# Second layer's MLP: the last four single tiles of the first chunk as seven half-size products

## The chip, the core and the metric

The kernel runs on one core of a Trainium2 chip. TensorE (PE) multiplies and writes to PSUM, VectorE (DVE) and ScalarE (ACT) do elementwise work, GpSimd (POOL) computes a little and issues transfers, SyncE (SP) issues transfers. The metric is the device time of one execution in microseconds; the kernel before takes 854.51 us, the median of three runs (853.74 to 854.65).

## What is computed

A decoder of two layers over 512 tokens of 1024 features, all in float32. Layer 0 mixes tokens by pooling, layer 1 by a gated unit; each then has an MLP of 4096 hidden features.

```python
for i in range(DEPTH):
    ...
    x = x + g1[:, None, :] * y
    h = modulate(rmsnorm(x, norm_mlp_g[i]), sh2, sc2)
    x = x + g2[:, None, :] * sq_relu_mlp(h, mlp_w1[i], mlp_w2[i])

def sq_relu_mlp(h, w1, w2):
    return jnp.square(jax.nn.relu(h @ w1)) @ w2
```

## The kernel before

**Products in three passes.** An operand is split into a high and a low half: ScalarE rounds it to the matmul type (`split`, L176; `parts`, L637), VectorE subtracts (L177, L638). `mm3` multiplies low by high, high by low and high by high (L187, L188, L190), so every product of two 128-row pieces costs three matmuls, all adding up in one PSUM bank.

**The MLP.** `mlp(i, ...)` handles the 4096 hidden features in four chunks of 1024, each in two quarters of 512. The up-projection `h @ w1` is made in one of two ways:

- A *single tile* (`f_prep`, `f_run`) makes 128 hidden features for all 512 tokens, 256 tokens at a time, over 8 pieces of the contraction. `put` applies relu (L678) and squares (L666).
- A *quarter by seven products* (`s_prep`, `s_run`) treats A (the normed tokens) as 2x2 blocks of 256 tokens by 512 input features, and B (a quarter of `w1`) as 2x2 blocks B11, B12, B21, B22 of 512 input by 256 hidden features. Instead of eight block products there are seven, of sums of blocks: product 1 is A11·B11, 2 is A12·B21, the others (5, 6, 3, 7, 4) use sums. Each has 2 x 4 x 3 matmuls of 256 columns. They run in the order 1, 5, 6, 3, 7, 2, 4.

Products 1, 6, 7 and 4 add up in one bank (`IN_X`, `XS`); 5 and 3 in a second and 2 in a third (`ZS`). After 1, 6 and 5 ScalarE copies the unfinished bank to `g` (L823); after 2, 3 and 7 VectorE combines bank and `g` (L826, L828, L830), then relu (L831) and square (L666).

The weights of a quarter are four loads of 512 KB (`blk`, SP's queue) into tiles of `w4`, which has three buffers. VectorE adds blocks (L787) for products 5 and 6; the sums for 7 and 4 are accumulating transfers on POOL's queue (L782). Each product's weight is then split (L176, L177).

The operands of 5, 6, 3 and 7 are sums of A's blocks: `a_sums(0)` to `a_sums(3)` make them in place in `h32` and split them into `as` tiles (one in `hx`, two in the buffers of the residual `x0`, `x1`, which are spilled to memory before) and, for product 7, into the part of `hb` that holds A21.

**Order.** `units` lists the steps: single tiles ("f"), products ("s"), down-projection steps of a chunk ("p") and of the last chunk ("q"). The loop prepares up to four steps ahead (`ahead`, which limits weight tiles), starts the pieces of `extra` (modulation columns, each tied to a number in the list), runs a step on TensorE, and goes on. TensorE's order is written by hand; on the other engines the framework's scheduler fixes an order when the kernel is built, and each works through it in sequence. In chunks made by products the list has the products between the down-projection steps of the chunk before, so that a p step lies between any two products of the group 1, 6, 7, 4.

In layer 1, `first1` makes the first four tiles of chunk 0 together: the first 256 tokens of each, then the other 256, while the second half of the tokens is still being normed (`normed(1, 1, 1)`). Then come the single tiles 4 to 7, then the products of chunk 1. `a_sums(0)` to `a_sums(3)` are called after tiles 4, 5, 6 and 7.

Of the kernel before, what the change touches and what calls it, by code (L numbers as in the profile page):

```python
# [14 lines left out]
P = 128  # L15
D = 1024
S = 512
KD = D // P
# [27 lines left out]
def c_g(n, k):  # L46
    return 24 * n + 16 + k
# [34 lines left out]
def decoder_kernel(ctx: ExitStack, tc: tile.TileContext, xtok, vecs, rows, fgrow, ada0, adag, ada1, pool_w, w1s, w1, w1f, w1b, w2, w2e, w_v, w_u, w_o, wsT, lnp, bs, out):  # L82
# [40 lines left out]
    mods = [cp.tile([P, 48], F32, name=f"mods{i}") for i in range(2)]  # L123
# [33 lines left out]
    def raw4(src):  # L157
        r = w4.tile([P, D], F32, name="raw", tag="w4")
        nc.sync.dma_start(r, src)
        return r  # L160
# [9 lines left out]
    def split(r, n=1):  # L170

        h, l = wpair()
        latest[0] = h
        for q in range(n):
            c = slice(D // n * q, D // n * (q + 1))
            A.activation(h[:, c], r[:, c], AF.Copy)  # L176
            V.tensor_tensor(l[:, c], r[:, c], f32(h[:, c]), ALU.subtract)  # L177
        return h, l
# [60 lines left out]
    def spread_cols(cols, name):  # L239

        po = bank("pb")[0:KD, 0:P]
        T.transpose(po, cols, ident)
        r = sm.tile([KD, P], F32, name="line", tag="line", bufs=1)
        A.activation(r, po, AF.Copy)
        line = dram.tile([KD, P], F32, name=name)
        G.dma_start(line, r)
        gb_[0] = big.tile([P, D], F32, name="gb", tag="gb")
        G.dma_start(gb_[0], line.rearrange("(o k) p -> o (k p)", o=1).to_broadcast([P, D]))
# [26 lines left out]
    with (  # L275
# [14 lines left out]
        m = band.rearrange("p n g w -> p (n g) w")  # L290
        G.affine_select(out=m, in_=m, compare_op=ALU.is_ge, fill=0.0, base=0, pattern=[[0, 8], [1, W]], channel_multiplier=-1)
        for g in range(4):
            m = band[:, :, g]
# [288 lines left out]
        for op in WORK.split():  # L582
            on_v, op = op.endswith("V"), op.rstrip("V")
            kind, d = op.rstrip("0123456789"), [int(c) for c in op if c.isdigit()]
# [42 lines left out]
    ORDER = (1, 5, 6, 3, 7, 2, 4)  # L627
# [10 lines left out]
        V.tensor_tensor(o[1], a, f32(o[0]), ALU.subtract)  # L638


    FROM = (2, 1)

    def mlp(i, first, extra, last, ending):

# [2 lines left out]
        with (  # L647
# [37 lines left out]

            def f_prep(u):
                c, f = u
                return split(raw4(w1[8 * c + f] if i == 0 else w1f[8 * c + f]))

            def f_run(u, w):  # L690
                c, f = u
# [41 lines left out]
            def a_sums(step):  # L733


                def a(r, j):
                    return h32[0][:, 4 * j : 4 * j + 4, 256 * r : 256 * r + 256]

                def operand(pool, tag):
                    t = pool.tile([P, 2, 4, 256], F32R, name="as", tag=tag)  # L740
                    return t[:, 0], t[:, 1]

                def minus(o, p, q):
                    V.tensor_tensor(o, p, q, ALU.subtract)

                first, half = slice(0, 256), slice(256, 512)
                if step == 0:
                    sums_a.update({1: H(slice(0, 4), first), 2: H(slice(4, 8), first), 4: H(slice(4, 8), half)})
                    shift(hx, LINE - GAP)
                    minus(a(1, 1), a(1, 0), a(1, 1))  # L750
                    m, o = 5, operand(hx, "hx")
                elif step == 1:
                    minus(a(1, 1), a(1, 1), a(0, 0))
                    m, o = 6, operand(big, "x0")
                elif step == 2:
                    minus(a(0, 0), a(0, 0), a(1, 0))
                    V.tensor_tensor(a(1, 1), a(1, 1), a(0, 1), ALU.add)
                    m, o = 3, operand(big, "x1")
                else:
                    m, o = 7, H(slice(0, 4), half)  # L760
                parts(o, a(0, 0) if m == 7 else a(1, 1))
                sums_a[m] = o
# [2 lines left out]

            def quad_at(c, j):

                return 2 * (c - FROM[i]) + j + i * 2 * (4 - FROM[0])

            def blk(c, j, r, n):  # L770
                if (c, j, r, n) not in blks:
# [212 lines left out]
                    ending()  # L984

            done = first(put)
            units = [("f", (0, f)) for f in range(done, 8)]
            for c in range(3):
                if c + 1 < FROM[i]:
                    fs, lead, step = [("f", (c + 1, f)) for f in range(8)], 3, (1, 1, 1, 1, 0, 1, 0)  # L990
                else:
                    fs, lead, step = [("s", (c + 1, j, m)) for j in range(2) for m in ORDER], 2, (1, 2, 3, 2, 2, 2, 0)
                units += fs[0:lead]
                fs = fs[lead:]
                for m, n in zip(ORDER2, step):
                    units.append(("p", (c, m)))
                    units += fs[0:n]
                    fs = fs[n:]
# [7 lines left out]

            def ahead(n):

                if i == 0 and ("s", (FROM[0], 0, 1)) not in units[: n + 5]:
                    return min(n + 3, len(units))  # L1010
                m, s = n + 1, items(*units[n])
                while m < len(units) and m < n + 5:
                    s += items(*units[m])
                    if s > 5 and m > n + 1:
                        break
                    m += 1
                return m

            ready = {}
            extra, at = list(extra), 0  # L1020
            for n, (kind, u) in enumerate(units):
                for m in range(n, ahead(n)):
                    if m not in ready:
                        ready[m] = prep[units[m][0]](units[m][1])
                while at < len(extra) and extra[at][0] <= n:
                    extra[at][1]()
                    at += 1
                if i == 0 and n in A_PARTS:
                    a_parts(A_PARTS.index(n))
                narrow[:] = [units[n + 1 : n + 2] and (units[n + 1][0] in "sf" or i and units[n + 1] == ("q", (1, NT - 1)))]  # L1030
                run[kind](u, ready[n])
                if i and kind == "f":
                    a_sums(u[1] - 4)
                if u == (3, 1, 4):
                    reload()

# [66 lines left out]
    def modulation_late(q, n, get, wait=4):  # L1103

        r = []
        return [(n, lambda: r.append(ada_load(ada1[q], get))), (n + wait, lambda: ada_tile(*column_at(q), r[0], True))]
# [20 lines left out]
    with (  # L1127
# [39 lines left out]
        u, gt, wu = {}, {}, {}  # L1167
# [100 lines left out]
            V.tensor_scalar(X(t)[:, S:c0], X(t)[:, S:c0], r, None, ALU.mult)  # L1268
            nc.sync.dma_start(out[t, :, 1], X(t)[:, S:D])

    ex = [x for q in range(8) for x in modulation_late(48 + q, 8 + 5 * q, late_gb if q == 0 else get_gb)]
    ex += [(58, lambda: spread_cols(mods[1][:, c_g(1, 0) : c_g(1, 0) + KD], "gain1"))]
    mlp(1, first1, ex, last1, lambda: None)


# [11 lines left out]
def _lay_out(inp):  # L1287
    import numpy as np

    def f(name):  # L1290
        return np.asarray(inp[name], dtype=np.float32)

    def cols(v):
        return v.reshape(-1, P).T

    def fmajor(w, ct):

        return w.reshape(KD, P, -1, ct).transpose(2, 1, 0, 3).reshape(-1, P, KD * ct)

    def halves(w):  # L1300

        return w.reshape(4, 2, P, 2, S).transpose(3, 0, 2, 1, 4)

    order = _ada_columns()
    d = {}
    d["xtok"] = f("x")[0].reshape(NT, P, D)
    adab = f("ada_b").reshape(2, 48, P)[:, order]
    d["vecs"] = np.concatenate([cols(v) for v in (f("c"), adab, f("norm_mix_g"), f("norm_mlp_g"))], axis=1)
    d["rows"] = np.stack([f("c")[0], adab[0, 16:24].reshape(-1), f("pool_scale")[0]])
    d["fgrow"] = f("final_g")  # L1310
    aw = f("ada_w").reshape(2, D, 48, P)[:, :, order]

    v0 = aw[0].transpose(1, 2, 0)
    d["ada0"] = np.concatenate([v0[0:16], v0[24:40]] + [v0[16 + 2 * g : 18 + 2 * g] for g in GT])
    d["adag"] = aw[0][:, 16:24].reshape(2, 4, P, 4, 256).transpose(3, 0, 2, 1, 4)[GM]
    d["ada1"] = np.concatenate([v0[40:48], aw[1].transpose(1, 2, 0)])
    d["pool_w"] = f("pool_w")[0].reshape(8, P, 256).transpose(1, 0, 2)
    w1 = f("mlp_w1")
    d["w1s"] = w1[0].reshape(KD, P, -1)[:, :, 0 : P * SWEEP]
    d["w1"] = fmajor(w1[0][:, : 2 * D], P)  # L1320
    d["w1f"] = fmajor(w1[1][:, :D], P)

    w1b = np.concatenate([w1[0][:, 2 * D :], w1[1][:, D:]], axis=1)
    d["w1b"] = w1b.reshape(2, 4, P, 10, 2, 256).transpose(3, 0, 4, 2, 1, 5).reshape(10, 2, 2, P, D)

    w2 = f("mlp_w2").reshape(2, 4, 2, 4, P, 2, S)
    d["w2"] = w2[:, 0:3].transpose(0, 1, 2, 5, 4, 3, 6)
    d["w2e"] = np.stack([halves(w[3 * D :]) for w in f("mlp_w2")])
    win = f("sgu_w_in")[0]
    d["w_v"] = halves(win[:, D:])  # L1330
    d["w_u"] = fmajor(win[:, :D], P)
    d["w_o"] = halves(f("sgu_w_out")[0])
    d["wsT"] = f("sgu_w_s")[0].transpose(2, 0, 1)
    d["lnp"] = np.concatenate([f("sgu_ln_g")[0], f("sgu_ln_b")[0]])
    d["bs"] = f("sgu_b_s")[0].reshape(-1)
    return {k: np.ascontiguousarray(v) for k, v in d.items()}
# [17 lines left out]
```

## Time and profile before

| what | value |
|---|---|
| median of three runs | 854.51 us |
| profiled execution, its own time | 854.5 us |
| its span, first to last instruction | 852.6 us |
| granted TensorE clock, mean | 0.997 |
| matmuls | 5116 |
| moved by DMA | 182.34 MB, mean 214 GB/s |

The profile gives busy times of the engines, the chain of work that ended last, who waited for whom, and the timeline, all in microseconds from the start of the span. Matmuls overlap in the pipeline: a row's duration is longer than the distance from one matmul's start to the next, and that distance is what one costs. Buffer numbers are left out of the names: `po` and `pm` are PSUM banks, `wh` and `wl` the halves of a weight, `raw` a loaded weight block, `h` the normed tokens (`h32`), `hb` their halves, `as` the halves of a sum of A's blocks, `g` hidden features. SPq and POOLq are transfers issued by SP and POOL.

### The profile page before, as it was taken

The page shows a single profiled execution, that of the slowest core. Times are in us where ns is not written, and L with a number is a line of the kernel's source. Part 1 is how long each engine was busy: PE and PEld are TensorE (multiplying, and loading weights), DVE is VectorE, ACT ScalarE, POOL GpSimd, SP SyncE. Part 2 cuts the span into 40 slices and gives each one's busy share as a digit, 9 for nine tenths or more (in the row PEclk, how much of TensorE's full clock was granted, in tenths as well). Part 3 has the DMA queues.
Part 4 walks back from the last instruction along what each step waited for, and adds up shares of the span by engine and source line. Part 5 has one row for each costly group of instructions (what it writes and reads, how often), then busy time and mean ns, then how long its engine had stood idle before and what let it go on. Part 6 is the DMA issues. An engine that isn't in the chain of part 4 may idle for free.

```text
span 852.6 us, 13079 instructions
## 1 busy us (share of the span) xinstructions
PE 839.5 (98%) x5116; PEld 747.5 (88%) x5116; DVE 686.2 (80%) x914; ACT 484.8 (57%) x716; POOL 65.5 (8%) x89
## 2 busy tenths in 40 slices
PE   8999999999999999999999999999999999999996
PEld 7778899998999998888888888999999999999885
DVE  6889897688898988767897866777788988887855
ACT  5286875565656577247333226666766666566521
POOL 3000000010101110010020001010101000111001
PEclk9999999999999999999999999999999999999998
DMA  9959955788898776724745636947888788786302
GB/s 351 417 226 324 347 191 179 222 203 216 215 283 231 224 205 224 269 97 165 264 168 172 217 129 221 322 94 197 205 247 217 218 212 244 180 178 230 129 25 98
DMA packets 43218, 182.34 MB, mean 214 GB/s; under 512 B 4859, under 2 KB 5011, under 8 KB 36118
## 3 DMA queue, kind: packets, MB, share of 16 engines
q1 hardware_dynamic: 35282, 137.72, 44.1%
q0 software_dynamic: 7440, 41.43, 24.0%
q10 hardware_dynamic: 436, 2.37, 0.8%
q8 instruction: 40, 0.66, 0.3%
q14 instruction: 20, 0.16, 0.1%
HBM read 175.19 MB, written 6.30 MB: 213 GB/s over the span
## 4 chain that ended last, share of the span: by engine, by line
PE 92%; DMA 4%; ACT 1%; DVE 1%; issue 1%; SPq 0%; POOLq 0%; POOL 0%; DVEq 0%; ACTq 0%
PE po L187 17%; PE po L190 17%; PE po L188 17%; PE pm L188 12%; PE pm L190 12%; PE pm L187 12%; DMA wh<-in_ada 2%; DMA wl<-in_ada 1%; DMA ada<-in_adag 1%; PE po L1192 1%; ACT sq L315 1%; PE px L1073 1%; PE po L611 0%; PE po L614 0%; PE po L612 0%
## 5 line engine op out<-in xcount | busy, mean ns | idle before, releaser
L187 PE MATMUL po<-hb,wl 128*128 128x256 f32 (+1 forms) x697 | 204.8, 294 | 0.2 <-DVE wl L177 0.2
L188 PE MATMUL po<-hb,wh 128*128 128x256 f32 (+1 forms) x696 | 204.1, 293 | 0.0
L190 PE MATMUL po<-hb,wh 128*128 128x256 f32 (+1 forms) x696 | 204.0, 293 | 0.0
L177 DVE TENSOR_TENSOR wl<-raw,wh 128x1024 fp32r<-128x1024 f32 (+1 forms) x122 | 145.5, 1195 | 45.5 <-ACT wh L176 45.2
L176 ACT ACTIVATE wh<-raw 128x1024 fp32r<-128x1024 f32 (+1 forms) x122 | 126.0, 1038 | 91.8 <-PE pm L190 42.3
L187 PEld LDWEIGHTS po<-hb,wl 128*128 128x128 f32 x697 | 130.9, 188 | 4.7 <-DVE wl L177 0.6
L190 PEld LDWEIGHTS po<-hb,wh 128*128 128x128 f32 x696 | 130.7, 188 | 4.1
L188 PEld LDWEIGHTS po<-hb,wh 128*128 128x128 f32 x696 | 130.8, 188 | 3.9
L190 PE MATMUL pm<-wh,oh 128*128 128x512 f32 (+1 forms) x375 | 131.1, 367 | 0.0
L188 PE MATMUL pm<-wl,oh 128*128 128x512 f32 x336 | 130.9, 390 | 0.0
L187 PE MATMUL pm<-wh,ol 128*128 128x512 f32 x336 | 130.8, 389 | 0.0
L190 PEld LDWEIGHTS pm<-wh,oh 128*128 128x128 f32 x375 | 70.4, 188 | 14.8
L215 DVE SCALAR_TENSOR_TENSOR ada<-ada,cb 128x1024 f32<-128x1024 f32 x56 | 68.1, 1218 | 10.1 <-DMA ada<-in_ada 8.7
L187 PEld LDWEIGHTS pm<-wh,ol 128*128 128x128 f32 x336 | 63.1, 188 | 11.8
L188 PEld LDWEIGHTS pm<-wl,oh 128*128 128x128 f32 x336 | 63.0, 188 | 11.6
L177 DVE TENSOR_TENSOR wl<-bt,wh 128x1024 fp32r<-128x1024 f32 x48 | 58.3, 1220 | 15.9 <-ACT wh L176 15.9
L187 PE MATMUL po<-as,wl 128*128 128x256 f32 x240 | 66.6, 278 | 0.0
L188 PE MATMUL po<-as,wh 128*128 128x256 f32 x240 | 66.4, 277 | 0.0
L190 PE MATMUL po<-as,wh 128*128 128x256 f32 x240 | 66.3, 276 | 0.0
L176 ACT ACTIVATE wh<-bt 128x1024 fp32r<-128x1024 f32 x48 | 50.4, 1058 | 20.5 <-PE pm L190 10.7
L177 DVE TENSOR_TENSOR wl<-b,wh 128x1024 fp32r<-128x1024 f32 x36 | 43.6, 1222 | 16.1 <-ACT wh L176 16.0
L1050 ACT ACTIVATE tmp<-x 128x512 f32<-128x512 f32 (+1 forms) x25 | 15.3, 612 | 61.9 <-DVE x L1046 56.1
(220 smaller groups left out, 1558.1 us busy)
## 6 DMA issues: line engine op xcount, KB each, us to landing
ada<-in_ada SPq DMA_DIRECT2D x72, 512.0 KB, 4.7
raw<-in_w1b SPq DMA_DIRECT2D x40, 512.0 KB, 5.3
b<-in_w SPq DMA_DIRECT2D x18, 1024.0 KB, 6.8
bt<-in_w POOLq DMA_DIRECT2D x16, 1024.0 KB, 8.8
raw<-in_w1b POOLq DMA_DIRECT2D x20, 512.0 KB, 5.7
raw<-in_w2e SPq DMA_DIRECT2D x16, 512.0 KB, 3.9
bt<-in_w SPq DMA_DIRECT2D x6, 1024.0 KB, 6.0
b<-in_w POOLq DMA_DIRECT2D x6, 1024.0 KB, 9.4
```

Source lines behind the costliest of these rows:

```text
L176: A.activation(h[:, c], r[:, c], AF.Copy)
L177: V.tensor_tensor(l[:, c], r[:, c], f32(h[:, c]), ALU.subtract)
L187: T.matmul(o[:, c], wl, mh[:, c], start=first and not c.start, stop=False, **kw)
L188: T.matmul(o, wh, ml, start=False, stop=False, **kw)
L190: T.matmul(o[:, c], wh, mh[:, c], start=False, stop=last and c.stop is None, **kw)
L215: V.scalar_tensor_tensor(r, r, 1.0, cb, ALU.mult, ALU.mult, accum_out=pmv[i, b][:, j : j + 1])
L315: A.activation(j, X(t)[:, c], AF.Square, scale=D**-0.5, accum_out=out)
L1050: A.activation(tmp, xt, AF.Square, scale=D**-0.5, accum_out=s[:, len(cs) : len(cs) + 1])
L1073: T.transpose(px[:, 256 * q + P * r : 256 * q + P * r + P], xs[r][:, P * (k + q) : P * (k + q) + P], ident)
L1192: T.matmul(po[:, tok[t]], vt[t][:, ch, c0 : c0 + P], wb[:, 0, hd], start=True, stop=True)
```

## The change

In layer 1, the single tiles 4 to 7 of chunk 0 are replaced by the seven products of that chunk's second quarter. `FROM` now counts quarters made by other means (4 in layer 0, as before 2 chunks; 1 in layer 1, before 1 chunk), and the weight tables follow. `a_sums(0)` and `a_sums(1)` are called before the list starts, `a_sums(2)` and `a_sums(3)` after its first two steps. The list of layer 1 is three steps longer (seven for four), and the numbers to which the modulation pieces are tied are raised by three.

```diff
-    FROM = (2, 1)
+    FROM = (4, 1)
...
-                return split(raw4(w1[8 * c + f] if i == 0 else w1f[8 * c + f]))
+                return split(raw4(w1[8 * c + f]))
...
-                return 2 * (c - FROM[i]) + j + i * 2 * (4 - FROM[0])
+                return 2 * c + j - FROM[i] + i * (8 - FROM[0])
...
-            units = [("f", (0, f)) for f in range(done, 8)]
+            units = [("s", (0, 1, m)) for m in ORDER] if i else [("f", (0, f)) for f in range(done, 8)]
             for c in range(3):
-                if c + 1 < FROM[i]:
+                if 2 * (c + 1) < FROM[i]:
...
-                if i == 0 and ("s", (FROM[0], 0, 1)) not in units[: n + 5]:
+                if i == 0 and ("s", (2, 0, 1)) not in units[: n + 5]:
...
             extra, at = list(extra), 0
+            if i:
+                a_sums(0)
+                a_sums(1)
             for n, (kind, u) in enumerate(units):
...
                 run[kind](u, ready[n])
-                if i and kind == "f":
-                    a_sums(u[1] - 4)
+                if i and n < 2:
+                    a_sums(n + 2)
...
-    ex = [x for q in range(8) for x in modulation_late(48 + q, 8 + 5 * q, late_gb if q == 0 else get_gb)]
-    ex += [(58, lambda: spread_cols(mods[1][:, c_g(1, 0) : c_g(1, 0) + KD], "gain1"))]
+    ex = [x for q in range(8) for x in modulation_late(48 + q, 11 + 5 * q, late_gb if q == 0 else get_gb)]
+    ex += [(61, lambda: spread_cols(mods[1][:, c_g(1, 0) : c_g(1, 0) + KD], "gain1"))]
...
-    d["w1f"] = fmajor(w1[1][:, :D], P)
+    d["w1f"] = fmajor(w1[1][:, :S], P)
...
-    w1b = np.concatenate([w1[0][:, 2 * D :], w1[1][:, D:]], axis=1)
-    d["w1b"] = w1b.reshape(2, 4, P, 10, 2, 256).transpose(3, 0, 4, 2, 1, 5).reshape(10, 2, 2, P, D)
+    w1b = np.concatenate([w1[0][:, 4 * S :], w1[1][:, S:]], axis=1)
+    d["w1b"] = w1b.reshape(2, 4, P, 11, 2, 256).transpose(3, 0, 4, 2, 1, 5).reshape(11, 2, 2, P, D)
```

## The prediction

> **What bounds the kernel now.** I read the page first (busy shares, granted clock, the chain that ended last), then TensorE's own waits in the second layer's MLP, then the stretch of the four single tiles by engine, and last the timelines of VectorE, ScalarE and the queues around it.
>
> ```profile
> span 852.6 us, 13079 instructions
> PE 839.5 (98%) x5116; PEld 747.5 (88%) x5116; DVE 686.2 (80%) x914; ACT 484.8 (57%) x716; POOL 65.5 (8%) x89
> PEclk9999999999999999999999999999999999999998
> PE 92%; DMA 4%; ACT 1%; DVE 1%; issue 1%; SPq 0%; POOLq 0%; POOL 0%; DVEq 0%; ACTq 0%
> ```
>
> TensorE is busy in 98% of the span, holds 92% of the chain, and its clock is full. TensorE's waits from 520 to 640 us are one row:
>
> ```profile
> PE po L187 <- DVE wl L177: 0.2, 1, 0.2
> ```
>
> So nothing but matmuls sets the time there: a matmul taken away shortens the kernel by its spacing, and a wait put in lengthens it. The spacing, from the chain in order of time (start, us, what); the same line comes back after three matmuls:
>
> ```profile
> 549.66 0.11 PE po L190
> 550.00 0.11 PE po L190
> ```
>
> 0.34 us for three 128x256 matmuls: 0.113 us each, though one row lasts 0.28. The four tiles lie between these two rows of TensorE's timeline (first matmul of tile 4; first of the next chunk's first product):
>
> ```profile
> 549.61 0.28 PE L187 MATMUL po<-hb,wl 128*128 128x256 f32 x1
> 571.37 0.28 PE L187 MATMUL po<-hb,wl 128*128 128x256 f32 x1
> ```
>
> 21.76 us, 192 matmuls of 0.113. The busy times in that stretch (PE, PEld, DVE, ACT, POOL, each with its count; then clock, DMA share, GB/s):
>
> ```profile
> 549.50:571.30 21.80, 21.80 (x195) 21.80 (x194) 15.45 (x14) 13.45 (x19) 1.71 (x2) 1.00 0.47 128
> ```
>
> VectorE has 6.4 us free, ScalarE 8.4. That is the cover the change draws on.
>
> **The change part by part.** *Removed.* A single tile issues 2 x 8 x 3 = 48 matmuls, a product 2 x 4 x 3 = 24. 192 become 168: 24 x 0.113 = **-2.72 us**. Seven products of 2.72 us, if none waits, start at 549.61 (product 1), 552.33 (5), 555.05 (6), 557.77 (3), 560.49 (7), 563.21 (2) and 565.93 (4), and end at 568.65.
>
> *Added.* Three more weight splits (seven for four), two sums of weight blocks on VectorE (L787), two accumulating transfers on POOL's queue, three copies of unfinished products on ScalarE (L823) and three additions on VectorE (L826, L828, L830). The sums of A's blocks are the same, earlier. Durations:
>
> ```profile
> 548.70 1.22 DVE L744 TENSOR_TENSOR h<-h 128x1024 f32<-128x1024 f32 x1
> 549.84 1.22 DVE L177 TENSOR_TENSOR wl<-raw,wh 128x1024 fp32r<-128x1024 f32 x1
> 550.97 1.22 DVE L638 TENSOR_TENSOR as<-h,as 128x1024 fp32r<-128x1024 f32 x1
> 596.92 0.67 DVE L830 TENSOR_TENSOR g<-g,po 128x512 f32<-128x512 f32 x1
> ```
> ```profile
> 542.93 1.06 ACT L176 ACTIVATE wh<-raw 128x1024 fp32r<-128x1024 f32 x1 [3.46 <-DMA raw<-in_w1f]
> 543.90 1.04 ACT L637 ACTIVATE as<-h 128x1024 fp32r<-128x1024 f32 x1
> 546.27 0.62 ACT L666 ACTIVATE g<-g 128x512 f32<-128x512 f32 x1
> 546.79 0.59 ACT L678 ACTIVATE g<-po 128x512 f32<-128x512 f32 x1
> 577.01 0.60 ACT L823 ACTIVATE g<-po 128x512 f32<-128x512 f32 x1 [0.85 <-PE po L190]
> ```
>
> Back to back, 1024 columns take VectorE 1.14 us from start to start and ScalarE 0.96; 512 columns take ScalarE 0.52. VectorE gains 5 x 1.14 + 3 x 0.6 = 7.5 us against 6.4 free, in a stage that is to be 2.7 shorter; ScalarE 3 x 0.96 + 3 x 0.52 = 4.4. VectorE is over-full there unless it works ahead, so I follow both queues in the order in which the changed program issues them.
>
> *Two waits that the single tiles didn't have.* Products 1, 6, 7 and 4 add up in one PSUM bank. After 1 and after 6 ScalarE copies the bank out, and VectorE reads it after 7: the next of the four can't start before that read. In the other chunks a down-projection step stands between any two of them; in the new first chunk at most one other product does. And the blocks of a weight have three buffers: the fourth block (B21) is loaded into the buffer of B22, only when B22 is split.
>
> *VectorE up to product 6.* Its place before the stage:
>
> ```profile
> 538.99 1.30 DVE L638 TENSOR_TENSOR hb<-h,hb 128x512 fp32r<-128x512 f32 x2 [0.66 <-ACT hb L637]
> 540.32 1.22 DVE L744 TENSOR_TENSOR h<-h 128x1024 f32<-128x1024 f32 x1
> 544.03 1.23 DVE L177 TENSOR_TENSOR wl<-raw,wh 128x1024 fp32r<-128x1024 f32 x1 [2.48 <-ACT wh L176]
> 545.17 1.22 DVE L638 TENSOR_TENSOR as<-h,as 128x1024 fp32r<-128x1024 f32 x1
> ```
>
> The sums can't begin before 540.3, when the second half of the tokens is normed; the first weight block lands at 542.9 in either kernel, for its load has the old one's place, size and wait. From 545.17 VectorE then works without a break: low half of operand 5, weight sum 5, two differences of A, low half of weight 5, low half of operand 6, weight sum 6, a sum of A, low half of operand 7, low half of weight 6. Weight 5 is ready at 545.17 + 4 x 1.14 + 1.22 = 550.95, in time for 552.33. Weight 6 is the tenth: 545.17 + 9 x 1.14 + 1.22 = **556.65**, wanted at 555.05.
>
> *ScalarE up to product 6.* The high half of weight 6 needs weight sum 6, done at 545.17 + 6 x 1.14 + 1.22 = 553.23. Behind it stand a square, the high halves of weights 3 and 7, and only then the copy of product 1: 553.27 + 0.96 + 0.52 + 2 x 0.96 = 556.67, done at 557.27. Product 6 starts at 557.3 instead of 555.05: **+2.3 us**, most of it the copy behind the splits. Bounds: 1.6 (VectorE alone) to 2.5. Operand 3 (VectorE's third piece behind weight 6) is done at 545.17 + 12 x 1.14 + 1.22 = 560.07, when product 6 ends: **+0.1**.
>
> *Product 7.* B22 is split at 557.8 and SP issues B21 then. ScalarE's next two operations are the high halves of weights 2 (B21) and 4 (an accumulating transfer issued at 556.7), and the copy of product 6 stands behind both. What 512 KB take to land, each row from a window with that issue alone:
>
> ```profile
> raw<-in_w1b SPq DMA_DIRECT2D x1, 512.0 KB, 3.3
> raw<-in_w1b SPq DMA_DIRECT2D x1, 512.0 KB, 4.8
> raw<-in_w1b SPq DMA_DIRECT2D x1, 512.0 KB, 5.7
> raw<-in_w1b POOLq DMA_DIRECT2D x1, 512.0 KB, 5.6
> raw<-in_w1f SPq DMA_DIRECT2D x1, 512.0 KB, 8.3
> ```
>
> 3.3 with nothing beside it, 4.8 and 5.7 with others in flight, 8.3 under several 1 MB loads. Here one accumulating transfer was issued 1.2 us before and one load follows 1.1 us later: I take 4.6, nearest to 4.8. B21 lands at 562.5, the two splits take until 564.4, the copy until 565.0: product 7 starts at 565.1 where TensorE is free at 562.8: **+2.3**. With 3.3 the accumulating transfer (556.7 + 5.6 = 562.3) ends last: 563.95, +1.15. With 5.7: +3.4.
>
> *Product 4.* VectorE's subtraction after product 7 (L830) is queued behind a weight sum of the next quarter, whose block takes B21's buffer: issued at 562.5 + 1.1 + 1.2 = 564.9, landed 3.3 to 4.8 later, plus 1.14 and 0.67: 570.0 to 571.5, where TensorE is free at 565.1 + 5.44 = 570.5. 0 to +1.0; I take **+0.3** (4.0 us, between the two rows).
>
> *At nothing.* Four loads of 512 KB replace four; the additions L826 and L828 and the squares are on no product's path; the new start numbers of the modulation pieces (11 and 61 for 8 and 58) keep their places in a list that is three longer; the weight table only changes its cut. The down-projection step that follows wants its weights at 573.2 + 5.44 = 578.7; VectorE is through with them five pieces behind L830, near 576.5: were those 2 us gone, each us later would cost one.
>
> *Sum.* -2.72 + 2.3 + 0.1 + 2.3 + 0.3 = +2.3 us. The profiled execution took 854.5 us (span 852.6 and 1.9 around it), as the median of the three runs, 854.51: **856.8 us**. With every cost at its low end +0.1 (-2.72 + 1.6 + 0.1 + 1.15), at its high end +4.3 (-2.72 + 2.5 + 0.1 + 3.4 + 1.0).
>
> **The rivals.** *All hidden, 851.8 us.* TensorE runs the seven products through and keeps the 2.72. For it: it doesn't wait anywhere in this MLP now, and its products there have the same copies. Against it: there other work stands between products that share a bank, and VectorE's ten pieces alone miss product 6 by 1.6 us. It decides if VectorE starts the chain some 2 us earlier, which the row at 538.99 speaks against. *One stall, 854.2 us.* Product 6 waits, but B21 is there early, as blocks are elsewhere: -2.72 + 2.4. Against it: B21's buffer. *Crowded loads, about 861 us.* B21 takes 8.3 instead of 4.6: product 7 loses 3.7 more, 860.5, and the next block adds some. It speaks against this that the DMA share in that stretch was 0.47. *The clock drops, about 859.5 us.* TensorE's longest pauses would be 2.3 to 2.5 us. A pause of 1.73 us in this trace left the clock at 1.00:
>
> ```profile
> 29.02 1.35 PE L431 MATMUL pg<-ada,cab 128*128 128x256 f32 x5 [1.73 <-DMA ada<-in_adag]
> 27.00:29.00 2.00, 0.30 (x2) 0.00 (x0) 2.00 (x4) 0.51 (x2) 0.00 (x0) 1.00 1.01 415
> ```
>
> Should a longer one halve it for one product, that product takes 2.7 us more. [...]
>
> **How the numbers follow.** Forecast 0.72, all hidden 0.11, one stall 0.07, crowded 0.06, clock 0.04. A measurement tells about 0.2% (1.7 us) from no change. Of the forecast's 0.72 I put 0.08 below +1.7, where the loads land in 3.3 to 3.8. Faster 0.11; within 0.2% 0.07 + 0.08 = 0.15; slower 0.64 + 0.06 + 0.04 = 0.74. The forecast's own range is 854.6 to 858.8; with one stall and the clock's case taken in, 854.2 to 859.6, which leaves out all hidden and crowded, 0.17.
>
> **What would show it.** 24 fewer matmuls, and in TensorE's waits two rows of about 2.3 us, both on ScalarE's copy (L823), for products 6 and 7; if the one at product 6 names a low half of a weight (L177) instead, VectorE set it. On ScalarE's timeline an idle time of about 3 us ahead of a split (L176), ended by the load of B21. Product 4 within 1 us, ended by L830. From the next chunk on every step shifted by one constant. Wrong, if TensorE's row of waits stays empty, if the shift is undone further on, or if the loss lies in another stage.

## The result and the profile after

| | before | after |
|---|---|---|
| median of 5 runs each, side by side (lowest to highest), us | 854.51 (853.72 to 856.12) | 858.81 (857.51 to 859.41) |
| ratio, 95% interval | | 1.0042 [1.0031, 1.0053] |
| profiled execution: time (span), us | 854.5 (852.6) | 857.5 (855.5) |

By the ratio the changed kernel is slower by 3.6 us (2.6 to 4.6); the medians lie 4.3 us apart. The page of the changed kernel, its first two lines of text and the shares of the chain that ended last:

```profile
span 855.5 us, 13056 instructions
PE 839.2 (98%) x5092; PEld 746.6 (87%) x5092; DVE 692.8 (81%) x922; ACT 488.5 (57%) x722; POOL 67.3 (8%) x91
...
PE 88%; DMA 6%; DVE 2%; ACT 2%; issue 1%; SPq 1%; POOL 0%; POOLq 0%; DVEq 0%; ACTq 0%
```

24 matmuls are gone and TensorE is busy for as long as before (839.2 for 839.5): most of what they freed came back as slower matmuls, and waits lie on top. TensorE's waits from 520 to 640 us (total, times, longest), and its first matmul of product 5 and of the next quarter's product 5:

```profile
PE po L187 <- ACT g L823: 3.8, 2, 2.1
```
```profile
552.12 0.28 PE L187 MATMUL po<-as,wl 128*128 128x256 f32 x1
577.22 0.28 PE L187 MATMUL po<-as,wl 128*128 128x256 f32 x1
```

Where the kernel before had one wait of 0.2, there are two of 2 us, both on ScalarE's copy. From product 5 to product 5 it takes 25.10 us. That is the length of the stage, as one product of 2.72 stands ahead of each end; the four single tiles took 21.76. So the stage costs **+3.34 us**; the span is 2.9 longer. The rows ahead of product 6, on VectorE, ScalarE and TensorE (start, length, idle time before it and what ended that):

```profile
555.28 3.48 DVE L177 TENSOR_TENSOR wl<-raw,wh 128x1024 fp32r<-128x1024 f32 x3
```
```profile
554.61 1.99 ACT L176 ACTIVATE wh<-raw 128x1024 fp32r<-128x1024 f32 x2
556.51 0.57 ACT L823 ACTIVATE g<-po 128x512 f32<-128x512 f32 x1
```
```profile
557.13 0.39 PE L187 MATMUL po<-as,wl 128*128 128x256 f32 x1 [2.13 <-ACT g L823]
```

The first of VectorE's three low halves is weight 6's, done near 556.5. Two high halves hold the copy of product 1 on ScalarE until 557.08, and product 6 starts 0.05 later, 2.3 us after product 5 ends (552.12 + 2.72). Product 7 in the chain of waits (start, us, what), and ScalarE's rows for it:

```profile
556.42 1.22 DVE wl L177
...
557.66 5.98 DMA raw<-in_w1b
...
563.66 2.01 ACT wh L176 x2
565.67 0.49 ACT g L823
...
566.21 0.39 PE po L187
```
```profile
563.66 2.01 ACT L176 ACTIVATE wh<-raw 128x1024 fp32r<-128x1024 f32 x2 [4.21 <-DMA raw<-in_w1b]
565.58 0.58 ACT L823 ACTIVATE g<-po 128x512 f32<-128x512 f32 x1
```

B22's split frees the buffer, B21 takes 5.98 us to land, two splits and the copy follow. Last, the stretch by windows (busy times of PE, PEld, DVE, ACT, POOL; then clock, DMA share, GB/s):

```profile
554.80:557.10 2.30, 0.20 (x2) 0.00 (x1) 2.30 (x3) 2.30 (x4) 0.30 (x1) 1.00 0.00 0
557.10:558.70 1.60, 1.57 (x13) 1.57 (x14) 1.60 (x3) 1.60 (x2) 0.54 (x1) 0.99 0.36 33
558.70:562.10 3.40, 3.40 (x18) 3.40 (x18) 3.40 (x4) 0.76 (x2) 0.00 (x0) 0.50 0.92 202
562.10:564.30 2.20, 2.20 (x21) 2.20 (x20) 0.07 (x1) 0.64 (x1) 0.00 (x0) 1.00 0.94 380
564.30:566.20 1.90, 0.20 (x2) 0.00 (x0) 1.44 (x2) 1.90 (x4) 0.00 (x0) 1.00 0.03 6
```

After the pause ahead of product 6 the clock was 0.50 for 3.4 us: a matmul started every 0.213 us, so 16 where 30 fit at 0.113 (the 18 of the row count those that reach over its edges). That slowed products 6 and 3, which would have ended at 562.6 (557.13 + 2 x 2.72), by some 1.8 us, and left 1.9 of the 3.6 us that product 7, set by B21, would have waited.

### The profile page after: what moved, and what is told of

The parts are those of the page before. It is cut to its first block, busy times and chain, and to the rows that moved or that the text cites. A ratio compares the mean times of both kernels' runs of the same rounds, so it can differ in the third digit from the quotient of the medians.

```text
span 855.5 us, 13056 instructions
## 1 busy us (share of the span) xinstructions
PE 839.2 (98%) x5092; PEld 746.6 (87%) x5092; DVE 692.8 (81%) x922; ACT 488.5 (57%) x722; POOL 67.3 (8%) x91
## 4 chain that ended last, share of the span: by engine, by line
PE 88%; DMA 6%; DVE 2%; ACT 2%; issue 1%; SPq 1%; POOL 0%; POOLq 0%; DVEq 0%; ACTq 0%
PE po L187 16%; PE po L190 16%; PE po L188 16%; PE pm L188 12%; PE pm L190 12%; PE pm L187 12%; DMA wl<-in_ada 2%; DMA wh<-in_ada 1%; DMA raw<-in_w1s 1%; PE po L1195 1%; PE px L1076 1%; DMA ada<-in_ada 1%; DMA raw<-in_w1b 1%; ACT sq L315 1%; ACT wh L176 0%
## 5 line engine op out<-in xcount | busy, mean ns | idle before, releaser
L187 PE MATMUL po<-hb,wl 128*128 128x256 f32 (+1 forms) x665 | 196.1, 295 | 1.7 <-ACT g L823 1.7
L188 PE MATMUL po<-hb,wh 128*128 128x256 f32 (+1 forms) x664 | 195.3, 294 | 0.0
L190 PE MATMUL po<-hb,wh 128*128 128x256 f32 (+1 forms) x664 | 195.1, 294 | 0.0
L177 DVE TENSOR_TENSOR wl<-raw,wh 128x1024 fp32r<-128x1024 f32 (+1 forms) x125 | 148.8, 1195 | 43.6 <-ACT wh L176 43.4
L176 ACT ACTIVATE wh<-raw 128x1024 fp32r<-128x1024 f32 (+1 forms) x125 | 128.9, 1038 | 91.7 <-PE pm L190 41.1
L187 PEld LDWEIGHTS po<-hb,wl 128*128 128x128 f32 x665 | 124.8, 188 | 6.3 <-ACT g L823 1.9
L190 PEld LDWEIGHTS po<-hb,wh 128*128 128x128 f32 x664 | 124.7, 188 | 4.1
L188 PEld LDWEIGHTS po<-hb,wh 128*128 128x128 f32 x664 | 124.8, 188 | 3.9
L187 PE MATMUL po<-as,wl 128*128 128x256 f32 x264 | 74.2, 281 | 2.1 <-ACT g L823 2.1
L188 PE MATMUL po<-as,wh 128*128 128x256 f32 x264 | 73.8, 279 | 0.0
L190 PE MATMUL po<-as,wh 128*128 128x256 f32 x264 | 73.6, 279 | 0.0
L187 PEld LDWEIGHTS po<-as,wl 128*128 128x128 f32 x264 | 50.3, 190 | 2.4 <-ACT g L823 2.3
```

Of the source, the lines that this page charges most:

```text
L187: T.matmul(o[:, c], wl, mh[:, c], start=first and not c.start, stop=False, **kw)
L188: T.matmul(o, wh, ml, start=False, stop=False, **kw)
L190: T.matmul(o[:, c], wh, mh[:, c], start=False, stop=last and c.stop is None, **kw)
```

## The experiments

Each kernel is the changed one with the edit shown. "Stage" is the length from product 5 to product 5 in its profile, to be read against 21.76 before; the ratio is to the kernel before, run on the same chip in the same comparison, where that took 855.6 to 856.1 us. A profile is one execution, the ratio is over several; executions of one kernel lie up to 4 us apart (the kernel before 854.1 to 858.0 in these comparisons), so a stage and a ratio need not agree to 1 us.

| kernel | stage, us | ratio to before, 95% |
|---|---|---|
| e1_again (no edit) | 24.54 | 1.0044 [1.0029, 1.0059] |
| e2_b21_own | 24.29 | 1.0031 [1.0020, 1.0042] |
| e5_fresh_bank | 23.98 | 1.0045 [1.0030, 1.0060] |
| e8_defer | 21.87 | 1.0167 [1.0151, 1.0182] |
| e9_short_3 | 22.98 | 1.0004 [0.9995, 1.0013] |
| e10_short_own_3 | 21.77 | 0.9992 [0.9983, 1.0001] |
| e3_p_between | 23.9 without the step put in | 1.0016 [1.0007, 1.0025] |
| e4_both | 24.0 without the step put in | 1.0012 [1.0002, 1.0022] |
| e13_own_late | 22.80 | 1.0000 [0.9991, 1.0010] |
| e13_short_own_late_3 | 21.64 | 1.0000 [0.9991, 1.0008] |
| e15_copy_first | 24.46 | 1.0035 [1.0023, 1.0048] |
| e19_in_order | 20.76 | 1.0144 [1.0125, 1.0163] |

**The changed kernel once more** (e1_again).

> The changed kernel once more, unedited. In its first profile (857.5 us, the lowest of its five runs) TensorE paused 2.3 us ahead of product 6 and 2.0 us ahead of product 7, and the granted clock was 0.50 for 3.4 us after the first pause only; that slow stretch lay in time that product 7 spent waiting for B21 anyway. Theory 'queues' (product 6 waits for ScalarE's copy, product 7 for B21's buffer): the same two pauses again, 857.5 to 858.5 us unless a clock drop falls where nothing hides it. Rival 'clock' (the halved clock sets the loss): slow stretches after both pauses in a profile of a run near 859, that is 1.6 us more than the first profile for a second stretch.

TensorE's waits (of over 0.2 us), two pieces of the chain and one window:

```profile
PE po L187 <- ACT g L823: 4.8, 2, 3.3
```
```profile
558.16 5.89 DMA raw<-in_w1b
...
566.08 0.49 ACT g L823
```
```profile
563.10:566.60 3.50, 0.26 (x3) 0.07 (x1) 1.43 (x2) 2.49 (x3) 0.00 (x0) 1.00 0.49 193
```

Here the clock stayed at 1.00, through a pause of 3.4 us, and the profiled execution takes 858.0 us beside 857.5: product 7 starts when B21 has come, however fast products 6 and 3 ran. In these two executions the clock is not where the loss comes from. For those without a trace that is open. The five of this run have a mean granted clock of 0.998, 0.996, 0.995, 0.992 and 0.994 and take 858.01, 858.61, 858.92, 859.30 and 859.86 us; the kernel before has 0.997 on average, and its times do not follow the clock. So up to 2 us of the slower executions, an estimate from the 1.9 between these five, may be drops that nothing hides.

**B21 in its own buffer** (e2_b21_own).

```diff
-                    blks[c, j, r, n] = raw4(w1b[quad_at(c, j), r, n])
+                    if (i, c, j, r, n) == (1, 0, 1, 1, 0):
+                        blks[c, j, r, n] = ada_load(w1b[quad_at(c, j), r, n], get_gb)
+                    else:
+                        blks[c, j, r, n] = raw4(w1b[quad_at(c, j), r, n])
```

> B21 of the new quarter gets a buffer of its own (the free gain tile), so its load no longer waits for B22's split. Queues: the copy of product 6 no longer waits for B21; what is left is the accumulating transfer for weight 4 (issued at 556.7, 5.6 to 5.9 us), so product 7 starts near 564.3 instead of 566.2: 1.5 to 2 us less than the changed kernel, about 857 us. Rival 'clock': the pause ahead of product 6 and the slow stretch behind it stay, and without the wait for B21 they are what sets product 7 (564.2): about the same 857, but then the chain of waits names TensorE's slow matmuls and no transfer. Rival 'over-full VectorE': no change, 858.8, since VectorE's work is the same.

Product 7's wait is gone, product 6's grew. TensorE's wait, the transfer that stopped ScalarE (issue, KB, us to landing) and ScalarE behind it:

```profile
PE po L187 <- ACT g L826: 3.5, 1, 3.5
```
```profile
raw<-in_w1b POOLq DMA_DIRECT2D x1, 512.0 KB, 10.3
```
```profile
558.08 1.06 ACT L176 ACTIVATE wh<-raw 128x1024 fp32r<-128x1024 f32 x1 [3.53 <-DMA raw<-in_w1b]
559.05 0.58 ACT L826 ACTIVATE g<-po 128x512 f32<-128x512 f32 x1
```

The buffer was free early, so SyncE issued B21 ahead of one of the 1 MB loads of the down-projection. The 1 MB accumulating transfer that depends on that load went out at 547.0 instead of 542.3, and weight 7's transfer beside it took 10.3 us. ScalarE stood 3.5 us before weight 7's split, with the copy of product 1 behind it. The clock's drop is not hidden here: it was 0.50 for 3.41 us from 559.15 on, and product 6 took 4.19 us where product 7 of the changed kernel, which follows a pause at full clock, takes 2.85. Products 3 and 7 follow without a wait, so some 1.3 us of this stage are the clock's; to that extent the rival 'clock' was right. The earlier load and the drop together cost most of what was saved. 1.5 to 2 us less than the changed kernel were forecast; the ratio is lower by 0.0011, 0.9 us, which the intervals do not tell from nothing.

**A bank of its own for product 6** (e5_fresh_bank). Product 6 starts a new bank; product 1 is thereby left out of three of the quarter's four output blocks.

```diff
-                start, stop = m in (1, 5, 2), m in (4, 3, 2)
+                start, stop = m in (1, 5, 2) or (i, c, j, m) == (1, 0, 1, 6), m in (4, 3, 2)
```

> Product 6 of the new quarter starts a fresh PSUM bank, so it doesn't wait for the copy of product 1; product 1 is left out of three of the quarter's four output blocks. Queues: product 6 then waits for the low half of its weight alone, 1.6 to 1.8 us instead of 2.3; product 7 still waits for B21, so the time stays that of the changed kernel, 858.8 within 0.5. Rival 'clock': if the shorter pause spares the clock, 1.6 us less; if the clock falls all the same, no change. Rival 'over-full VectorE': no change.

```profile
556.14 0.35 PE L187 MATMUL po<-as,wl 128*128 128x256 f32 x1 [0.50 <-DVE wl L177]
565.63 0.39 PE L187 MATMUL po<-hb,wl 128*128 128x256 f32 x1 [3.28 <-ACT g L823]
```

Product 6 no longer waits for the copy, only 0.5 us for its weight (1.6 to 1.8 were expected; in this execution VectorE's pieces came 0.5 us earlier and TensorE 0.5 later than in the changed kernel's profile), and product 7 waits the whole rest for B21 and its copy. The ratio is that of the changed kernel: the first wait alone is worth nothing.

**The 1 MB loads later** (e8_defer). The down-projection's first two loads wait for a write that ScalarE makes from the latest split.

```diff
+                if (i, c) == (1, 0) and not chain:
+                    A.activation(t[:, 0, 0:1], f32(latest[0])[:, 0:1], AF.Copy)
                 nc.sync.dma_start(t, w2[i, c, r, n])
```

> The two 1 MB loads of down-projection weights that run ahead of the new quarter's blocks (issued near 527, landed at 538 and 541.5) are held back until the weights of a later step are split. Queues: B11 lands some 3 to 4 us earlier (539 instead of 542.7), VectorE's chain of ten pieces begins by as much earlier, and product 6 doesn't wait, or under 0.5 us; no slow clock behind it. Product 7 still waits for B21, now from a B22 that is split some 2.5 us earlier: about 2.3 to 3 us less than the changed kernel, 856 us. Rival 'over-full VectorE': the work is the same but begins earlier, the same sign, so this run tells only where the pause goes. Rival 'clock': the slow stretch goes with the pause; the gain over the changed kernel is at most 1.6 us beyond what B21 allows.

The stage lost its first wait and took 21.87 us. But the loads came too late for the steps that they feed; TensorE's waits from 520 to 640 us (those of over 0.2), with clock drops of 6.83 and 3.41 us behind the two longest (mean granted clock 0.991):

```profile
PE pm L187 <- ACT wh L176: 7.3, 2, 4.3
PE po L187 <- ACT g L823: 2.2, 1, 2.2
PE pm L188 <- DVE wl L177: 1.5, 2, 0.8
```

**Weights prepared two units ahead** (e9_short_3).

```diff
+                if i and n < 6:
+                    return n + 3
                 m, s = n + 1, items(*units[n])
```

> For the first six units of the second layer the weights are prepared only two units ahead instead of up to four, so that ScalarE's copies of products 1 and 6 are queued ahead of the weight splits that are not yet wanted. Theory (the waits of products 6 and 7 come from the order in ScalarE's queue, and behind it B21): product 6 waits for its own weight's low half on VectorE, about 1.6 us instead of 2.3; product 7 no longer stands behind B21's split; B21, issued near 557.7 and landing 6 us later, is wanted only by product 2, which then starts near 565.7 to 566 instead of 568.9. The stage costs -2.7 + 1.6 + 0.9 + 0.5 = about +0.3, against +3.3 in the changed kernel: about 855 us, 2.5 to 3 us less than the changed kernel. Rival (the buffer of B21 sets the end of the stage, whoever waits for it): product 4 or the next quarter takes over what product 7 gave back, and the time stays within 1 us of the changed kernel. What would show it: ScalarE's copy (L823) gone from TensorE's waits, a low half (L177) in its place.

```profile
PE po L187 <- DVE wl L177: 2.2, 2, 1.3
PE po L187 <- DVE g L830: 0.5, 1, 0.5
```

The copy is gone from TensorE's waits and low halves stand in its place, for product 6 (1.1 us) and for product 2, which needs B21; product 4 waits 0.5 for VectorE's subtraction of product 7. The edit changes when weights are prepared, and with it the order on ScalarE and on VectorE, and adds or removes no work. It takes 0.0038 of the ratio, 3.3 us, from the changed kernel, where 2.5 to 3 us were forecast. The stage is only 2.1 us shorter (1.6 beside e1_again); no drop of the clock follows its pauses, the longest 1.3 us, which may be the rest.

**Both, first form** (e10_short_own_3): the edits of e2_b21_own and e9_short_3.

> The short preparation of the kernel before, and B21 in a buffer of its own. Theory (two causes, ScalarE's order and B21's buffer): only product 6's wait for its weight is left, 1.6 us, as the late accumulating transfer that stopped ScalarE when B21 alone had its own buffer now stands behind the copy of product 1: the stage costs -2.7 + 1.6 + 0.3 = -0.8, about 853.5 to 854 us beside 854.5 of before. Rival (the second buffer takes SyncE's queue: its issue waits for the buffer and holds the loads behind it): weight 7 lands near 558 and the waits move on to products 7 and 4, 1 to 2 us each, and the time is that of e9_short_3 or more.

```profile
560.29 0.38 PE L187 MATMUL po<-as,wl 128*128 128x256 f32 x1 [1.52 <-ACT g L826]
```

Product 6 waits 0.4, product 7 not at all; product 3 waits 1.5 for the copy of product 5, which stands behind the split of the late weight 7. That is the rival's wait, on a product that it did not name. The time is near that of the kernel before: the interval, -1.5 to +0.1 us, holds the theory's -0.8 as well as no change, and the stage, 21.77 us for 21.76, speaks for the latter.

**A down-projection step between products 5 and 6** (e3_p_between), and with B21 in its own buffer (e4_both). The down-projection steps that follow are taken from `order` instead of `ORDER2`, and at product 4 weights are prepared two units ahead.

```diff
+                order = ORDER2
+                if i and c == 0:
+                    units.insert(2, ("p", (0, 1)))
+                    order, step = ORDER2[1:], (1, 2, 3, 2, 2, 2)
...
+                if units[n] == ("s", (0, 1, 4)):
+                    return n + 3
```

> The first down-projection step of the layer is moved from behind the seven products to a place between products 5 and 6; the buffers and the sums stay. Theory (the waits come because too little work stands between products that share a bank): the copy of product 1 and weight 6 have 5.4 us more, so product 6 doesn't wait, and B21 has as much more ahead of product 7; in exchange the down-projection step may wait up to 3 us for its own operand's split on VectorE, which is over-full there. The stage costs between -2.2 and +0.5, so 852.3 to 855 us. Rival (VectorE's amount of work sets the stage, not the order): the wait only moves to the down-projection step and the time stays within 1 us of the changed kernel's.

> The down-projection step between products 5 and 6, and B21 in a buffer of its own. Theory of the two causes: as e3_p_between, and what was left there ahead of product 7 is gone: at most 1 us less than e3_p_between. Rival (SyncE's queue is held by the issue for the second buffer): the accumulating transfer of weight 7 is late, near 558, but with 5.4 us more in hand product 7 does not notice, and the time is the same as e3_p_between's within 0.5 us.

TensorE's waits in e3_p_between (of over 0.2 us):

```profile
PE pm L187 <- DVE ol L638: 4.0, 2, 2.6
PE po L187 <- ACT g L823: 1.6, 1, 1.6
```

With the step between them product 6 waits for nothing, but the step waits 2.6 us for its own operand's low half, on VectorE, and product 7 still 1.6. The step after the stage waits 1.4 more. e3_p_between lies between its two theories: 0.0026 of the ratio, 2.2 us, below the changed kernel, and above the forecast. The distance between the products matters, and VectorE could not supply the step that was put there in time. In e4_both the step waits 0.5, but product 7 waits 2.3 for the copy of product 6, which stands behind the split of weight 4; that weight's accumulating transfer, issued at 557.1 behind one of 1 MB, took 10.5 us. The clock was then 0.50 for 3.41 us, and product 7 took 4.40 us instead of 2.72. So product 7 did wait, which neither theory said; the ratio, 0.0004 below e3_p_between's, fits both.

**B21 in its own buffer, loaded after the split of weight 5** (e13_own_late), and with weights prepared two units ahead (e13_short_own_late_3).

```diff
                 w = split(wb)
+                if (i, c, j, m) == (1, 0, 1, 5):
+                    blks[c, j, 1, 0] = ada_load(w1b[quad_at(c, j), 1, 0], late_gb)
```

> B21 again in a buffer of its own, but its load is issued only after the split of weight 5 (near 548), so that it no longer takes a place ahead of the layer's 1 MB loads; the long preparation of the changed kernel stays. Theory (two separate waits: ScalarE's order ahead of product 6, B21's buffer ahead of product 7): product 7 does not wait, product 6 waits 2.3 us as before, weight 7 lands near 554 to 556 and stops nobody. The stage costs -2.7 + 2.3 + 0.1 + 0.2 = about 0: the time of the kernel before within 0.7 us, so about 3 us less than the changed kernel. Rival (any further load in this stretch delays another one that is needed, as in e2_b21_own): the accumulating transfer of weight 7 takes 8 to 10 us, ScalarE stands before its split again and product 6 waits 3 to 4 us: about 857 to 858 us where the kernel before takes 855.

> The same late load of B21 into its own buffer, with the weights prepared only two units ahead. Theory of the two waits: both are gone but for weight 6's own low half on VectorE, 1.6 us; product 3, which waited 1.5 us in e10_short_own_3 behind the late weight 7, waits for nothing. The stage costs -2.7 + 1.6 + 0.3 = -0.8 to -1.1: ratio to the kernel before 0.9987 or less, the first version below it. Rival (VectorE has too much work for the shorter stage, whatever the loads do): what products 6, 3 and 7 do not wait, products 2 and 4 and the next quarter do, on VectorE (L177, L830), and the ratio is that of e10_short_own_3, 0.9992, or above.

Both take the time of the kernel before: the first as forecast (its one profiled stage is 1.0 longer), the second not below it, as its rival had it. But the waits are not those of either theory: in e13_own_late product 6 waits 1.5 instead of 2.3, and product 7, which was to wait for nothing, 1.7; the forecast time came about by luck in part. In e13_short_own_late_3 products 2 and 4 do not wait for VectorE, and product 7 waits 1.7. What is left, on ScalarE in e13_own_late:

```profile
562.86 1.06 ACT L176 ACTIVATE wh<-raw 128x1024 fp32r<-128x1024 f32 x1 [2.43 <-DMA raw<-in_w1b]
563.82 0.58 ACT L825 ACTIVATE g<-po 128x512 f32<-128x512 f32 x1
```

B21 is there, and now the copy of product 6 stands behind the split of weight 4, whose accumulating transfer is the next to land. The prediction named both transfers ahead of this copy; with the one early, the other holds it.

**The copy of product 6 ahead of weight 4's split** (e15_copy_first): e13_short_own_late_3, with weights prepared three units ahead from product 3 on, and

```diff
+        if behind is not None:
+            A.activation(h[:, 0:1], behind, AF.Copy)
```

in `split`, with `behind` a column of the block that the copy of product 6 writes.

> As e13_short_own_late_3, and the split of weight 4 is held behind ScalarE's copy of product 6 by a write of one column that reads the copied block. In e13_short_own_late_3 product 7 still waited 1.5 us, for that copy stood behind the split of weight 4, whose accumulating transfer landed at 561.7. Theory (a third wait of the same kind, on ScalarE's order): product 7 starts when product 3 ends, product 4 has its weight near 566.5 where it is wanted at 566.7, and the stage gains 1.3 to 1.5 us more: the ratio to the kernel before falls to about 0.9985, the stage from product 1 to the next quarter is 2 us shorter than in the kernel before. Rival (what one product does not wait, the next does: the accumulating transfer sets the end): product 4 waits 1 to 1.5 us on its weight's low half and the ratio stays at 1.000.

```profile
PE po L189 <- DVE g L834: 3.1, 1, 3.1
```
```profile
569.01 1.23 DVE L789 TENSOR_TENSOR raw<-raw 128x1024 f32<-128x1024 f32 x1
570.16 0.68 DVE L834 TENSOR_TENSOR g<-g,po 128x512 f32<-128x512 f32 x1
```

Product 7 waits for nothing, and product 4 waits 3.1 us for VectorE's subtraction of product 7, which the scheduler now placed behind the next quarter's low half and weight sum. Product 7's wait is gone, as the theory had it, but not the time: the ratio is 1.0035, 3 us above e13_short_own_late_3. The rival's sentence holds, at twice its price and with another cause; it named the low half of product 4's weight and a ratio of 1.000.

**Every order fixed by data** (e19_in_order): e15_copy_first with the next quarter's first split held behind weight 4's, and its weight sum behind the subtraction of product 7, through an operand `one` that is always 1; at products 7 and 2 weights are prepared two units ahead instead of three:

```diff
+                    if (i, c, j) == (1, 0, 1):
+                        held["one"] = sm.tile([P, 1], F32, name="one", tag="one", bufs=1)
+                        V.tensor_scalar(held["one"], t[:, 0, 0:1], 0.0, 1.0, ALU.mult, ALU.add)
...
+                        V.scalar_tensor_tensor(t, t, held["one"], b(*CHAIN[m]), ALU.mult, ALU.add)
```

> What e15_copy_first showed to be left: product 4 waited 3.2 us for VectorE's subtraction of product 7, which stood behind the low half and the weight sum of the next quarter, and these behind loads that landed at 563.9 and 566.0. Here the next quarter's first split is held behind the split of weight 4, and its weight sum behind that subtraction (each by an operand that the earlier operation writes). Theory (every wait left in the stage is an order on ScalarE or VectorE, none is the amount of work): no product waits but product 6, 0.3 to 1.8 us; the stage from product 1 to the next quarter takes 19.4 to 20.9 us where the kernel before takes 21.8, and the ratio to the kernel before is 0.997 to 0.999. Rival (VectorE has too much work for seven products in this stage): the wait moves on once more, to the next quarter's products 5 and 6 on their weights' low halves (L179), 1 to 2 us, and the ratio stays within 0.0008 of 1.

TensorE's one wait from 500 to 700 us, and the ends of the stage:

```profile
PE po L189 <- DVE wl L179: 1.2, 1, 1.2
```
```profile
559.28 0.28 PE L189 MATMUL po<-as,wl 128*128 128x256 f32 x1
580.04 0.28 PE L189 MATMUL po<-as,wl 128*128 128x256 f32 x1
```

In the stage the theory holds: 20.76 us, 1.0 below the kernel before, and only product 6's wait for VectorE is left, as the prediction's lower bound for it said (1.6; product 6 starts 1.4 late here). Yet the kernel takes 11 to 12 us more than the kernel before, where 1 to 3 us less were forecast, and loses it outside the stage, in the MLPs of both layers. From 120 to 220 us, with the same instructions in the same order on every engine, in e15_copy_first and then in e19_in_order:

```profile
120.00:220.00 100.00, 100.00 (x651) 90.87 (x650) 77.40 (x81) 59.68 (x77) 7.09 (x8) 1.00 0.70 195
```
```profile
120.00:220.00 100.00, 100.00 (x630) 89.55 (x629) 76.53 (x79) 58.62 (x75) 6.51 (x8) 1.00 0.68 195
```

Both at full clock without a wait, 630 matmuls against 651. The same 1200 matmuls, from the 801st to the 2000th of the program, take 186.1 us instead of 181.9, 2.3% longer. What the edit changes there is where buffers lie, for `one` adds a word to each partition of a pool that is laid out ahead of others. That the places are the reason is argued from this, not shown. A version with the order of e19_in_order and the old places is the one that the runs point to; it wasn't tried.

## Why the prediction was right, and where it was off

The forecast was 856.8 us for 858.81, on the right side, with both waits in their places and for the causes that it gave. The loss was larger than forecast, +3.34 us in the stage for +2.3, and the median lies at the upper edge of the forecast's own range, 854.6 to 858.8.

- *Matmuls removed, -2.72.* 5116 became 5092. Right.
- *Product 6, +2.3.* Measured +2.29; start 557.13 for 557.3, low half 556.5 for 556.65, released by the copy behind the splits. Right in size and cause.
- *Product 3, +0.1, and product 7, +2.3.* Together +3.64. The mis-sized term is B21's load: 5.98 us, and 5.89 in the second profile, for the 4.6 chosen; the bound at 5.7 was nearer. Issue (557.66 for 557.8) and the 2.5 us from landing to start were right, so 5.98 - 4.6 - 0.14 = 1.2 accounts for the start at 566.21 instead of 565.1. An accumulating transfer, issued 0.9 us before, and a load, issued 1.1 us behind, were in flight beside it; which of them slowed it more than was allowed for isn't shown. The row of 3.3 us had been read as a load with nothing beside it; another load of 512 KB was issued 1.1 us behind that one too. In e1_again, at full clock, product 3 starts 2.85 us after product 6: it hardly waits.
- *Product 4, +0.3.* It did not wait. VectorE's subtraction was done at 571.42, near the 570.7 forecast, but TensorE, held up by product 7, came to product 4 only at 571.78:

```profile
570.74 0.68 DVE L830 TENSOR_TENSOR g<-g,po 128x512 f32<-128x512 f32 x1
```

- *Sum.* -2.72 + 2.29 + 3.64 + 0.13 = +3.34 for the +2.3 forecast; the 0.13 are product 7's own, whose first matmuls after the pause start slower (2.85 us for 2.72). The profiled execution was the fastest of the five; the 1.3 us between it and the median have no trace.
- *The clock rival.* The clock did drop, after a pause of 2.3 us that the forecast had taken to be harmless. That was the author's estimate: the longest of TensorE's waits in the trace of before was 1.7 us, and no run had shown what a pause of 2.3 does. The rival's 2.7 us assumed half the clock for one whole product; measured were 0.50 for 3.41 us, and some 1.8 us lost in products 6 and 3. In the profiled execution even that lengthened nothing: the drop fell where product 7 would have waited anyway, and e1_again, without it, takes as long. With B21 early there is no such wait, and in e2_b21_own the drop cost some 1.3 us. What it adds in the executions without a trace is open.
- *"At nothing".* The down-projection step after the stage did not wait, and from the next chunk to 800 us every matmul comes 3.12 us later than in the kernel before; 0.2 us came back at the end.
- *The two causes.* ScalarE's order is the first: e9_short_3, which alters only the order of preparation, took back 3.3 us by the ratio (2.1 in the stage). B21's buffer is the second: with order left as it was, e13_own_late took back about as much (2.3 in the stage). They do not add up, for with either gone the next landing transfer or VectorE's queue sets the start of a product: e13_short_own_late_3 has both, its stage is 1.2 us shorter than with one of them, and its ratio, known to 0.0009, does not show even that. One more order fixed moved the wait to product 4, and all fixed made the stage 1.0 us shorter than before instead of 2.7, with 1.4 of the rest in VectorE's ten pieces ahead of product 6.

## What to carry to other kernels

Here 24 matmuls less on the bounding engine cost 3.6 us by the ratio, because the products that replaced them did not find their weights and banks ready. So follow each in-order queue, and ask which split or copy stands behind a transfer that has not landed. Removing one such wait tells little until the next one in line is known, and an earlier or later load can move the others: in e2_b21_own the 1 MB transfer went out 4.7 us later, and weight 7's took 10.3 us. When an experiment adds a buffer, check the matmul rate in a stage that it should not touch: in e19_in_order it was 630 matmuls in 100 us for 651.

## What the runs showed of the hardware

- *The clock dropped after some pauses and not after longer ones.* Pauses of 2.3 us (the changed kernel) and 2.4 (e4_both) were followed by 0.50 for 3.41 us, one of 3.2 us in e8_defer by 0.50 for 6.83 us, while 3.4 us (e1_again and e5_fresh_bank) left the clock at 1.00. The drop of e4_both:

```profile
569.16:572.57 3.41, 3.33 (x15) 3.33 (x16) 3.17 (x3) 0.97 (x2) 0.00 (x0) 0.50 0.46 138
```

So the length of the pause does not tell which of these was followed by a drop; what does isn't shown.

- *512 KB took 3.3 to 10.5 us to land, longer in these cases with more in flight beside them.* A load took 3.3 us with one load issued 1.1 us behind it (before), and 5.9 to 6.0 with an accumulating transfer of 512 KB ahead of it as well (e1_again and the changed kernel); an accumulating transfer took 5.5 to 5.9 (before and the changed kernel) and, behind one of 1 MB, 10.3 (e2_b21_own), 10.4 (the changed kernel, issued at 579.1) and 10.5 (e4_both).
- *The same matmuls took 2.3% longer at full clock and in the same order.* In e19_in_order the 801st to the 2000th took 186.1 us for 181.9. Its edit adds one word to a pool; that the places of the buffers are the reason is not shown.
